# Loads and stores of a decoder block's weight parts on GpSimd's queue, and a buffer of their own for the gate rows

## The chip, the cores and the metric

One core of a Trainium2 chip runs the program. Times are device microseconds. The metric is the time of one execution, taken as the median over runs. TensorE is called PE, VectorE DVE, ScalarE ACT, GpSimd POOL and SyncE SP. Each of them takes its instructions in the order in which the built program has them; a transfer (DMA) is issued by the engine in whose order it stands, and an instruction that waits holds up those behind it on the same engine.

## The reference

The kernel computes one decoder layer on a sequence of 1024 tokens with a width of 1024, all in float32. What matters here:

```python
mod = jax.nn.silu(c) @ w_ada + b_ada            # shift, scale, gate
h = rms_norm(x, norm_gain) * (1.0 + scale) + shift
q, k, v, z_a, u, z_b, m_a, m_b = split(h @ w_in)
p_a = (stick_breaking_attention(q, k, v) * silu(z_a)) @ w_branch_a
p_b = (pool(u) * silu(z_b)) @ w_branch_b
out = (sigmoid(m_a) * p_a + sigmoid(m_b) * p_b) @ w_out
return rms_norm(x + gate * out, final_gain)
```

## The kernel before, in words

Each float32 product is made of three matmuls. An operand is split into a high part (a cast on ACT) and a low part (the operand less its high part, a subtraction on DVE or POOL), and high x high, high x low and low x high are added up in a PSUM bank. The normed input `hT` stays on the chip as high and low parts. A projection takes one tile of 128 columns of a weight (128 x 1024 numbers, 512 KB) and makes two groups of 24 matmuls, one for each half of the sequence, each into one of the two banks of the tag `pj`.

The stages follow one another on PE: maps and the projection u (to about 129 us), the values v (16 groups, to 218), the gate projection z_b, called wzb (8 tiles j = 0 to 7, two groups each, 218 to 317), the product with `w_branch_b` (seven products p1, p5, p6, p7, p4, p3, p2 of 48 matmuls each, to 394), attention mixed with the other projections (to about 1032), and the end with `w_branch_a` and `w_out`.

The projections of the attention stage use 40 tiles of `w_in`. For the first 8 the low part is made when they are used, by POOL (L118). For the other 32, the numbers 8 to 39, the low part is made ahead of time, in the stages u, v, wzb and the products, and kept in DRAM as `wl_d`; attention loads it from there. `make_lo` (L142 to L160) does this for one tile at a time: a load of the raw tile (L149, the tile `l8_raw` to `l39_raw`, tag `lraw`), the cast of it (L152, ACT, into `l_hi`, one buffer), the low part in place of the raw tile (L153, DVE), and the store (L154). A buffer of `lraw` can take the next load when its store has landed. 18 tiles are made in u and v, from the pool of buffers `vp`, which has three buffers of `lraw` and is closed at the end of v. 14 tiles are made from the pool `pb`: the code asks for four of them in the loop over wzb (`LO_ZB`) and for ten behind the seven products (`LO_PB`).

The order of each engine is not the order of the code: a scheduler places the instructions, by its own estimate of their times, in all stages in which the code doesn't pin them. So all 14 tiles of `pb` stand among the instructions of wzb.

In wzb, for each half of each tile j, ACT takes the sigmoid of the bank (L663) and DVE multiplies it with the bank (L664), which is the last reader of the bank, and then with the pooled difference (L665). The group after the next on PE writes the same bank and so waits for L664. Also in this stage DVE makes the pooled differences (L556 to L573), the low parts of the weights of wzb (L118), sums and differences of `gb` (L669 to L672), the first operands of the products (L642, L654), and the gate: one row of `w_gate` for each j (tile `wg`, loaded by L680) is multiplied with silu(c) and summed (L681). silu(c) is made once, from `sg` and `gjunk` (L675 to L678). In the kernel before, `gjunk` and the eight `wg` use the buffers of `lraw`, three in all.

SP issues nearly all loads and stores: the weights of v (L580) and of wzb (L131), the pooled input u (L557), the stores of v (L611), `wg` (L680), the halves of `w_branch_b` (L648), and L149 and L154. ACT issues a few stores. POOL issues no transfers; between 67 and 390 us it has no instruction.

Of the kernel before, what the change touches and what calls it, by code (L numbers as in the profile page):

```python
# [9 lines left out]
F32 = mybir.dt.float32  # L10
# [5 lines left out]
P = 128  # L16
D = 1024
# [23 lines left out]
LO_ZB = (0, 1, 0, 1, 0, 1, 0, 1)  # L41
LO_PB = (1, 2, 1, 2, 1, 2, 1)
# [15 lines left out]
def block_kernel(ctx, tc, a, out):  # L58
    nc = tc.nc
    v, act, gp = nc.vector, nc.scalar, nc.gpsimd  # L60

    def pool(name, **kw):
        return tc.tile_pool(name=name, bufs=1, reuse_waits="tile", **kw)
# [9 lines left out]
    def bank(tag, name):  # L73
        return psp.tile([P, 512], F32, tag=tag, bufs=BANKS[tag], name=name)
# [8 lines left out]
    wl_d = dram.tile([5 * KB, P, D], F32, name="wl_d")  # L83
# [51 lines left out]
    tiles = []  # L135
# [6 lines left out]
    def make_lo(pl, n, bufs=3, later=False):  # L142

        rest = []
        for _ in range(n):
            i = next(early_lo)
            raw = pl.tile([P, D], F32, tag="lraw", bufs=bufs, name=f"l{i}_raw")
            hi = pl.tile([P, D], F32R, tag="lhi", bufs=1, name=f"l{i}_hi")
            nc.sync.dma_start(raw, a["w_in"][tiles[i]])  # L149

            def low(i=i, raw=raw, hi=hi):
                act.copy(hi, raw)  # L152
                v.tensor_sub(raw.bitcast(F32R), raw, hi.bitcast(F32))  # L153
                nc.sync.dma_start(wl_d[i], raw)  # L154

            if later:
                rest.append(low)
            else:
                low()
        return rest  # L160
# [27 lines left out]
    def project(ct, name, use, he, le):  # L188
        whl = load_w(a["w_in"][ct], name, he, le)
        for sh in range(2):  # L190
            ps = bank("pj", f"{name}_{sh}")
            mm3(ps, whl, (h_hi, h_lo), range(KB), hmov(sh))
            use(sh, ps)
# [18 lines left out]
    with pool("init") as init:  # L212
# [101 lines left out]
        wg, maps, halves = {}, {}, {}  # L314
# [239 lines left out]
    def load_u(j):  # L554
        u = dif.tile([P, S + 16], F32, tag="u", bufs=2, name=f"u{j}")
        v.memset(u[:, S:], 0.0)  # L556
        nc.sync.dma_start(u[:, :S], u_d[j])  # L557
        return u

    def make_d(j, u):  # L560
        win = WINDOWS[j // 2]
        cur, n, step = u, S + 16, 1
        while step < win:
            nxt = dif.tile([P, S + 16], F32, tag="win", bufs=2, name=f"win{j}_{step}")
            n -= step
            v.tensor_add(nxt[:, :n], cur[:, :n], cur[:, step:step + n])
            cur, step = nxt, 2 * step
        t0 = S - win + 1
        d = dif.tile([P, S], F32, tag="d", bufs=5, name=f"d{j}")
        v.scalar_tensor_tensor(d[:, :t0], cur[:, :t0], 1.0 / win, u[:, :t0], ALU.mult, ALU.subtract)  # L570
        tl = dif.tile([P, 16], F32, tag="tl", bufs=2, name=f"tl{j}")
        v.tensor_mul(tl[:, :win - 1], cur[:, t0:S], invn[:, 16 - win + 1:])
        v.tensor_sub(d[:, t0:], tl[:, :win - 1], u[:, t0:S])  # L573
        dhls[j] = d


    with pool("vp") as vp:
# [6 lines left out]
        for i in reversed(range(KB)):  # L584
            ps = bank("pj", f"u{i}_1")
            mm3(ps, whl[i], h, range(KB), hmov(1))
            use[i](1, ps)
            make_lo(vp, 1)
# [6 lines left out]
        for hf in range(2):  # L595
            if hf == 0:
                wv.append([load_wv(1, k2) for k2 in range(4)])
            for sb in range(8):
# [18 lines left out]
                if 8 * hf + sb in DIFFS:  # L617
                    j = DIFFS[8 * hf + sb]
# [8 lines left out]
    pb = pbs.enter_context(pool("pb"))  # L627
# [11 lines left out]
    def b_op(src, name):  # L639
        hl = pb.tile([P, 2, 2, 512], F32R, tag="bhl", bufs=3, name=name)  # L640
        act.copy(hl[:, 0], src)
        v.tensor_sub(hl[:, 1], src, hl[:, 0].bitcast(F32))  # L642
        return hl
# [7 lines left out]
    def a_op(src, name):  # L651
        hl = wts.tile([P, 2, 2, 512], F32R, tag="whl", bufs=2, name=name)
        act.copy(hl[:, 0], src)
        v.tensor_sub(hl[:, 1], src, hl[:, 0].bitcast(F32))  # L654
        return hl

    for j in range(KB):
        if j not in dhls:
            make_d(j, load_u(j))

        def silu(sh, ps):
            z = gb[:, j, sh * 512:sh * 512 + 512]
            act.activation(z, ps, AF.Sigmoid)  # L663
            v.tensor_mul(z, ps, z)  # L664
            v.scalar_tensor_tensor(z, dhls[j][:, sh * 512:sh * 512 + 512], psc_v[:, j:j + 1], z, ALU.mult, ALU.mult)  # L665

        project(CZB + j, f"wzb{j}", silu, act, v)
        if j < 4:
            v.tensor_sub(t1[:, j], gb[:, j, 512:], gb[:, j, :512])  # L669
        else:  # L670
            v.tensor_sub(t2[:, j - 4], gb[:, j, 512:], t1[:, j - 4])
            v.tensor_sub(gb[:, j - 4, 512:], gb[:, j, 512:], gb[:, j - 4, 512:])  # L672
        make_lo(pb, LO_ZB[j])
        if j == 0:
            nc.sync.dma_start(sg, a["c_row"].broadcast_to([P, D]))  # L675
            gjunk = pb.tile([P, D], F32, tag="lraw", bufs=3, name="gjunk")
            act.activation(gjunk, sg, AF.Sigmoid)
            v.tensor_mul(sg, sg, gjunk)  # L678
        wg = pb.tile([P, D], F32, tag="lraw", bufs=3, name=f"wg{j}")
        nc.sync.dma_start(wg, a["w_gate"][j])  # L680
        v.scalar_tensor_tensor(wg, wg, 1.0, sg, ALU.mult, ALU.mult, accum_out=gate[:, j:j + 1])  # L681
        del dhls[j]
# [50 lines left out]
    def out_b(j, n, t):  # L733
        nc.sync.dma_start(pb_d[j][:, 512 * n:512 * n + 512], t)

    def copied(tag, bufs, j, src):
        t = sums.tile([P, 512], F32, tag=tag, bufs=bufs, name=f"{tag}_{j}")
        act.copy(t, src)
        return t

    def added(t, src):
        v.tensor_add(t, src, t)
        return t

    for n, (name, a_of, b_of) in enumerate(products):
        c = {"p5": "b", "p3": "b", "p2": "c"}.get(name, "a")
        if c not in chain:
            chain[c] = [bank((tb if c == "b" else ta)[j], f"{name}_{j}") for j in range(4)]
        ps = chain[c]
        for q in range(2):  # L750
            wl_, ml_ = a_op(a_of(q), f"{name}a{q}"), b_op(b_of(q), f"{name}b{q}")
            for j in range(4):
                for e in range(2):
                    for i, (w, m) in enumerate(((0, 0), (0, 1), (1, 0))):
                        mm(
                            ps[j], wl_[:, w, e, j * P:(j + 1) * P], ml_[:, m, e],
                            start=name in ("p1", "p5", "p2") and (q, e, i) == (0, 0, 0), stop=(q, e, i) == (1, 1, 2),
                                skip_group_check=True,
                        )
        for j in range(4):  # L760
            if name == "p1":
                keep["s1", j] = copied("s1", 4, j, ps[j])
            elif name == "p6":
                keep["s2", j] = copied("s2", 4, j, ps[j])
            elif name == "p7":
                out_b(j + 4, 1, added(copied("s3", 2, j, ps[j]), chain["b"][j]))
            elif name == "p4":
                out_b(j + 4, 0, copied("s4", 2, j, ps[j]))
            elif name == "p3":
                out_b(j, 1, added(keep["s2", j], ps[j]))  # L770
            elif name == "p2":
                out_b(j, 0, added(keep["s1", j], ps[j]))
        make_lo(pb, LO_PB[n])
    pbs.close()


# [295 lines left out]
    with pool("fin") as fin:  # L1072
# [14 lines left out]
        for sh in range(2):  # L1087
            sl = slice(sh * 512, sh * 512 + 512)
            ms = []
            for j in range(KB):  # L1090
# [9 lines left out]
                n = 0  # L1100
# [12 lines left out]
            for i in range(4):  # L1113
# [8 lines left out]
                for c_, cl in enumerate(pieces):  # L1122
                    w_ = cl.stop - cl.start
                    ps = bank(("z", "tr")[c_ % 2], f"o{sb}_{c_}")[:, :w_]
                    n = 0
# [85 lines left out]
```

## Time and profile before

| | us |
|---|---|
| median of 3 runs | 1214.39 (1213.62 to 1216.64) |
| the profiled execution | 1216.13 |
| its span, first to last instruction | 1214.4 |
| PE busy | 1193.9 (98%) |
| DVE busy | 796.0 (66%) |
| ACT busy | 549.3 (45%) |
| POOL busy | 168.8 (14%) |
| mean granted clock of PE | 0.996 |

A row of a timeline gives the start, the busy time, the engine, the line, the operation, the tiles (out<-in), the shapes and the count; the brackets give the idle time before it and what ended that. Instructions overlap a little, so the distance between two starts (1.14 for an operation over 1024 columns on DVE) is less than the busy time (1.22). In a row of stages the numbers are the length, the busy time and count of PE, weight loads, DVE, ACT and POOL, the granted clock, the busy share of the DMA engines and the GB/s. A row of transfers gives the issuer, the count, the size and the median time from issue to landing.

### The profile page before, as it was taken

To read this page: it belongs to the slowest core of one execution; us is meant where nothing else is said; L and a number is where in the kernel's file an instruction comes from. 1 tells how busy PE (TensorE), PEld (TensorE's weight loads), DVE (VectorE), ACT (ScalarE), POOL (GpSimd) and SP (SyncE) were. 2 spreads that over 40 slices of the span, in tenths; PEclk is the share of its full clock that TensorE was granted. 3 is DMA by queue.
4 is the path that set the end of the run, shared out by engine and by line. 5 is a ranking of instruction groups with operands and counts; after the bars stand their busy time and mean duration, and the time that the engine had idled before them with its cause. 6 is when DMAs were issued, how large, how long until landed. Compare 5 with 4: busy or idle time off the path is not lost.

```text
span 1214.4 us, 16128 instructions
## 1 busy us (share of the span) xinstructions
PE 1193.9 (98%) x5698; PEld 995.1 (82%) x5698; DVE 796.0 (66%) x1088; ACT 549.3 (45%) x1020; POOL 168.8 (14%) x352
## 2 busy tenths in 40 slices
PE   8999999998999999999999999999999999999997
PEld 7888788876888888888888888888888888888876
DVE  5754473696765186777858678686777753785643
ACT  5564231332453255655655655555655653232211
POOL 1000000000000333222222221222221210000001
PEclk9999999998999999999999999999999999999999
DMA  9648895687725732343534325353353235984622
GB/s 355 253 172 320 317 364 211 215 261 210 268 86 187 229 81 72 116 129 99 165 114 141 106 88 165 109 157 106 107 140 100 96 124 195 335 276 162 208 73 83
DMA packets 85699, 212.39 MB, mean 175 GB/s; under 512 B 10609, under 2 KB 24049, under 8 KB 83442
## 3 DMA queue, kind: packets, MB, share of 16 engines
q1 hardware_dynamic: 77410, 196.47, 49.3%
q10 hardware_dynamic: 8208, 14.88, 3.3%
q8 instruction: 45, 0.74, 0.2%
q14 instruction: 36, 0.29, 0.1%
HBM read 144.20 MB, written 50.34 MB: 160 GB/s over the span
## 4 chain that ended last, share of the span: by engine, by line
PE 83%; DMA 7%; DVE 5%; issue 2%; ACT 1%; POOL 0%; SPq 0%; POOLq 0%; DVEq 0%; ACTq 0%
PE p L103 43%; PE o L103 6%; PE av L103 6%; PE z L103 6%; PE wt L103 5%; PE v L103 5%; PE pa L103 5%; DMA wl_d<-l_raw 3%; PE ua L103 3%; PE wzb L103 2%; DMA l_raw<-in_w_in 2%; PE u L103 2%; PE wm L103 1%; DVE l_raw L153 1%; DMA m<-sb_d 1%
## 5 line engine op out<-in xcount | busy, mean ns | idle before, releaser
L103 PE MATMUL p<-hT,w 128*128 128x512 f32 x1920 | 479.7, 391 | 0.0
L103 PEld LDWEIGHTS p<-hT,w 128*128 128x128 f32 x1920 | 355.3, 188 | 73.8 <-DVE klo L103 0.2
L933 DVE TENSOR_TENSOR_SCAN om<-om 128x512 f32<-128x512 f32 (+7 forms) x128 | 175.5, 1371 | 123.8 <-ACT om L926 69.0
L926 ACT ACTIVATE om<-z 128x512 f32<-128x512 f32 (+2 forms) x192 | 94.6, 493 | 156.0 <-PE z L103 133.2
L952 ACT CAST wt<-wt 128x512 fp32r<-128x512 f32 (+1 forms) x160 | 88.2, 551 | 48.1 <-PE wt L103 47.9
L953 DVE TENSOR_TENSOR wt<-wt,wt 128x512 fp32r<-128x512 f32 (+1 forms) x160 | 99.3, 620 | 16.1 <-ACT wt L952 15.5
L103 PE MATMUL av<-wt,vv 128*128 128x512 f32 x320 | 106.4, 414 | 0.0
L931 POOL TENSOR_SCALAR_AFFINE_SELECT om<-om 128x128 f32<-128x128 f32 x128 | 57.3, 448 | 345.6 <-ACT om L926 286.2
L103 PE MATMUL wzb<-hT,wzb 128*128 128x512 f32 x384 | 91.3, 399 | 8.4 <-DVE gb L664 8.4
L103 DVE TENSOR_TENSOR be<-be,om 128x511 f32<-128x511 f32 (+7 forms) x128 | 95.2, 749 | 1.1 <-POOL be L931 0.7
L103 PEld LDWEIGHTS wzb<-hT,wzb 128*128 128x128 f32 x384 | 73.7, 193 | 25.8 <-DVE gb L664 10.3
L927 ACT ACTIVATE be<-z 128x512 f32<-128x512 f32 (+2 forms) x192 | 94.0, 490 | 0.0
L103 PE MATMUL pa<-ga,wa 128*128 128x512 f32 x384 | 89.9, 390 | 1.0 <-DVE s L1105 1.0
L103 PE MATMUL o<-wo,mhl 128*128 128x512 f32 (+1 forms) x408 | 89.6, 377 | 0.0
L103 PE MATMUL wt<-ident,be 128*128 128x128 f32 x576 | 89.4, 273 | 0.0
L103 PE MATMUL v<-wv,hT 128*128 128x512 f32 x384 | 88.1, 390 | 1.2 <-DVE vo L610 1.2
L103 PEld LDWEIGHTS v<-wv,hT 128*128 128x128 f32 x384 | 71.9, 188 | 17.2 <-DVE vo L610 2.3
L103 PEld LDWEIGHTS pa<-ga,wa 128*128 128x128 f32 x384 | 71.9, 188 | 16.7 <-issue 1.3
L103 PEld LDWEIGHTS o<-wo,mhl 128*128 128x128 f32 x408 | 73.5, 188 | 14.1
L103 PEld LDWEIGHTS wt<-ident,be 128*128 128x128 f32 x576 | 70.2, 141 | 11.6
L152 ACT CAST l_hi<-l_raw 128x1024 fp32r<-128x1024 f32 x32 | 33.7, 1052 | 80.5 <-DMA l_raw<-in_w_in 74.4
L153 DVE TENSOR_TENSOR l_raw<-l_raw,l_hi 128x1024 fp32r<-128x1024 f32 x32 | 39.2, 1224 | 44.1 <-ACT l_hi L152 43.9
(175 smaller groups left out, 1476.5 us busy)
## 6 DMA issues: line engine op xcount, KB each, us to landing
w_raw<-in_w_in SPq DMA_DIRECT2D x40, 512.0 KB, 4.5
l_raw<-in_w_in SPq DMA_DIRECT2D x32, 512.0 KB, 5.3
wl_d<-l_raw SPq DMA_DIRECT2D x32, 512.0 KB, 5.9
w<-wl_d SPq DMA_DIRECT2D x32, 512.0 KB, 3.8
v_d<-vo SPq DMA_DIRECT2D x16, 512.0 KB, 4.8
vv<-v_d SPq DMA_DIRECT2D x8, 1024.0 KB, 5.4
wa_raw<-in_w_branch_a SPq DMA_DIRECT2D x16, 512.0 KB, 4.7
wa<-in_w_mod SPq DMA_DIRECT2D x7, 1024.0 KB, 7.3
```

The source lines that it names most:

```text
L103: ins = op(*args, **kw)
L152: act.copy(hi, raw)
L153: v.tensor_sub(raw.bitcast(F32R), raw, hi.bitcast(F32))
L926: act.activation(om[:, b0:b0 + n], zp[:, :n], AF.Sigmoid, scale=-0.125)
L927: act.activation(be[:, b0:b0 + n], zp[:, :n], AF.Sigmoid, scale=0.125)
L931: gp.affine_select(out=tl[:, :P], in_=tl[:, :P], pattern=[[1, P]], compare_op=ALU.is_gt, fill=fill, base=0, channel_multiplier=-1)
L933: v.tensor_tensor_scan(om[:, :W], om[:, :W], om[:, :W], 1.0, ALU.mult, ALU.min)
L952: act.copy(wt[:, 0, :off], pt[:, :off])
L953: v.tensor_sub(wt[:, 1, :off], pt[:, :off], wt[:, 0, :off].bitcast(F32))
```

## The change

```diff
@@ make_lo
-            nc.sync.dma_start(raw, a["w_in"][tiles[i]])
+            gp.dma_start(raw, a["w_in"][tiles[i]])
...
-                nc.sync.dma_start(wl_d[i], raw)
+                gp.dma_start(wl_d[i], raw)
@@ the loop over wzb
-        make_lo(pb, LO_ZB[j])
+        make_lo(pb, LO_ZB[j], 2)
...
-            gjunk = pb.tile([P, D], F32, tag="lraw", bufs=3, name="gjunk")
+            gjunk = pb.tile([P, D], F32, tag="wg", bufs=1, name="gjunk")
...
-        wg = pb.tile([P, D], F32, tag="lraw", bufs=3, name=f"wg{j}")
+        wg = pb.tile([P, D], F32, tag="wg", bufs=1, name=f"wg{j}")
@@ behind each product
-        make_lo(pb, LO_PB[n])
+        make_lo(pb, LO_PB[n], 2)
```

L149 and L154 are issued by POOL in place of SP, in all 32 rounds. In `pb`, `lraw` has two buffers in place of three, and `gjunk` and the `wg` share one of their own; the space is the same. Line numbers stay as they are.

The scheduler places the instructions anew. PE's order is the same. On SP, at the start of wzb, before:

```order
L680 DMA wg0_1798<-in_w_gate 128x1024
L149 DMA l26_raw_1863<-in_w_in 128x1024
L680 DMA wg1_1869<-in_w_gate 128x1024
L680 DMA wg2_1934<-in_w_gate 128x1024
L131 DMA wzb4_raw_2022<-in_w_in 128x1024
L149 DMA l27_raw_1999<-in_w_in 128x1024
L557 DMA u7_2256<-u_d_78 128x1024
L154 DMA wl_d_79<-l26_raw_1863 128x1024
```

Now, at the same place, SP has the gate rows, the weights and u alone:

```order
L680 DMA wg0_1798<-in_w_gate 128x1024
L131 DMA wzb4_raw_2022<-in_w_in 128x1024
L680 DMA wg1_1869<-in_w_gate 128x1024
L557 DMA u7_2256<-u_d_78 128x1024
L680 DMA wg2_1934<-in_w_gate 128x1024
L131 DMA wzb5_raw_2102<-in_w_in 128x1024
L680 DMA wg3_2005<-in_w_gate 128x1024
```

POOL had nothing between L255 and the L118 of the first attention weights. It now has the loads and stores of the tiles, here from the first of `pb` on:

```order
L149 DMA l26_raw_1863<-in_w_in 128x1024
L149 DMA l27_raw_1999<-in_w_in 128x1024
L154 DMA wl_d_79<-l26_raw_1863 128x1024
L149 DMA l28_raw_2165<-in_w_in 128x1024
L154 DMA wl_d_79<-l27_raw_1999 128x1024
L149 DMA l29_raw_2335<-in_w_in 128x1024
L154 DMA wl_d_79<-l28_raw_2165 128x1024
L149 DMA l30_raw_2427<-in_w_in 128x1024
```

Load and store alternate: the load of a tile stands between the stores of the two tiles before it, and it goes on like this to l39. The next on POOL are the L118 of the first attention weights.

On DVE, at the end of wzb, before (`wzb6_1` is the bank of the second half of tile 6):

```order
L153 TENSOR_TENSOR l37_raw_2855<-l37_raw_2855,l37_hi_2856 128x1024
L153 TENSOR_TENSOR l38_raw_2861<-l38_raw_2861,l38_hi_2862 128x1024
L664 TENSOR_TENSOR gb_1725<-wzb6_1_2223,gb_1725 128x512
L665 SCALAR_TENSOR_TENSOR gb_1725<-d6_2185,vecs_89,gb_1725 128x512
L654 TENSOR_TENSOR p1a0_2357<-a11_0_2355,p1a0_2357 128x1024
L671 TENSOR_TENSOR t2_1727<-gb_1725,t1_1726 128x512
L672 TENSOR_TENSOR gb_1725<-gb_1725 128x512
L153 TENSOR_TENSOR l39_raw_2943<-l39_raw_2943,l39_hi_2944 128x1024
L664 TENSOR_TENSOR gb_1725<-wzb7_0_2277,gb_1725 128x512
L665 SCALAR_TENSOR_TENSOR gb_1725<-d7_2267,vecs_89,gb_1725 128x512
L664 TENSOR_TENSOR gb_1725<-wzb7_1_2305,gb_1725 128x512
```

And now:

```order
L153 TENSOR_TENSOR l37_raw_2855<-l37_raw_2855,l37_hi_2856 128x1024
L664 TENSOR_TENSOR gb_1725<-wzb6_1_2223,gb_1725 128x512
L665 SCALAR_TENSOR_TENSOR gb_1725<-d6_2185,vecs_89,gb_1725 128x512
L654 TENSOR_TENSOR p1a0_2357<-a11_0_2355,p1a0_2357 128x1024
L671 TENSOR_TENSOR t2_1727<-gb_1725,t1_1726 128x512
L672 TENSOR_TENSOR gb_1725<-gb_1725 128x512
L153 TENSOR_TENSOR l38_raw_2861<-l38_raw_2861,l38_hi_2862 128x1024
L664 TENSOR_TENSOR gb_1725<-wzb7_0_2277,gb_1725 128x512
L665 SCALAR_TENSOR_TENSOR gb_1725<-d7_2267,vecs_89,gb_1725 128x512
L153 TENSOR_TENSOR l39_raw_2943<-l39_raw_2943,l39_hi_2944 128x1024
L664 TENSOR_TENSOR gb_1725<-wzb7_1_2305,gb_1725 128x512
L665 SCALAR_TENSOR_TENSOR gb_1725<-d7_2267,vecs_89,gb_1725 128x512
```

l38 and l39 stand one group later; l26 stands at the start of the stage, right behind L678, where the first L681 stood. In between, from l28 to l39, one new L153 stands ahead of each L664 except that of wzb2_1. The eight L681 stand later than before, the last ahead of L664 of wzb5_0 in place of wzb3_0.

## The prediction

> **What bounds the kernel now.** I read the page first, then who waited for whom, then the timelines of PE and DVE, then the chain in order of time.
>
> ```profile
> span 1214.4 us, 16128 instructions
> PE 1193.9 (98%) x5698; PEld 995.1 (82%) x5698; DVE 796.0 (66%) x1088; ACT 549.3 (45%) x1020; POOL 168.8 (14%) x352
> ...
> q1 hardware_dynamic: 77410, 196.47, 49.3%
> q10 hardware_dynamic: 8208, 14.88, 3.3%
> ```
>
> PE is busy for 98% of the span, so what a change of queues can win is a part of the 20.5 us in which it is idle. The waits of PE say where those are, and its timeline says when.
>
> ```profile
> PE wzb L103 <- DVE gb L664: 8.4, 4, 4.4
> PE v L103 <- DVE vo L610: 1.2, 2, 1.0
> ```
>
> ```profile
> 217.99 38.24 PE L103 MATMUL wzb<-hT,wzb 128*128 128x512 f32 x168
> 257.73 5.74 PE L103 MATMUL wzb<-hT,wzb 128*128 128x512 f32 x24 [1.50 <-DVE gb L664]
> 264.79 11.17 PE L103 MATMUL wzb<-hT,wzb 128*128 128x512 f32 x48 [1.32 <-DVE gb L664]
> 277.14 16.79 PE L103 MATMUL wzb<-hT,wzb 128*128 128x512 f32 x72 [1.19 <-DVE gb L664]
> 298.29 19.35 PE L103 MATMUL wzb<-hT,wzb 128*128 128x512 f32 x72 [4.36 <-DVE gb L664]
> 317.48 11.17 PE L103 MATMUL p<-p1b,p1a 128*128 128x512 f32 x48
> ```
>
> The wzb stage has 16 groups of 24 matmuls. The first seven take 38.24, so 5.46 each, and 16 would take 87.4; the stage takes 317.48 - 217.99 = 99.5. Four waits make 8.4 of the difference. The last also costs clock: 72 matmuls take 16.79 before it and 19.35 after it, 2.6 more, while the granted clock (last number but two) falls.
>
> ```profile
> 256.00:288.00 32.00, 27.99 (x121) 22.30 (x120) 28.86 (x39) 11.68 (x14) 0.00 (x0) 1.00 0.72 181
> 298.00:302.00 4.00, 3.71 (x9) 2.94 (x10) 3.57 (x6) 1.32 (x2) 0.00 (x0) 0.50 0.92 304
> ```
>
> The waits of 1.2 to 1.5 left it at 1.00; the one of 4.36 halved it. All these waits end with L664 on DVE, which frees the bank. Why L664 is late stands in the chain in order of time and in DVE's timeline.
>
> ```profile
> 241.12 5.22 DMA wl_d<-l_raw
> 246.35 3.57 DMA l_raw<-in_w_in
> ...
> 250.00 1.06 ACT l_hi L152
> ...
> 251.08 0.14 DVE l_raw L153
> ```
>
> ```profile
> 227.07 1.23 DVE L678 TENSOR_TENSOR sg<-sg,gjunk 128x1024 f32<-128x1024 f32 x1 [1.34 <-ACT gjunk L677]
> 228.33 1.22 DVE L681 SCALAR_TENSOR_TENSOR wg<-wg,sg 128x1024 f32<-128x1024 f32 x1
> ...
> 229.70 0.69 DVE L664 TENSOR_TENSOR gb<-wzb,gb 128x512 f32<-128x512 f32 x1
> ...
> 235.18 1.22 DVE L153 TENSOR_TENSOR l_raw<-l_raw,l_hi 128x1024 fp32r<-128x1024 f32 x1
> ...
> 239.26 1.23 DVE L153 TENSOR_TENSOR l_raw<-l_raw,l_hi 128x1024 fp32r<-128x1024 f32 x1
> ...
> 243.95 1.22 DVE L118 TENSOR_TENSOR wzb<-wzb_raw,wzb 128x1024 fp32r<-128x1024 f32 x1
> 245.09 1.22 DVE L642 TENSOR_TENSOR p1b<-gb,p1b 128x1024 fp32r<-128x1024 f32 x1
> ```
>
> ```profile
> 313.57 1.22 DVE L153 TENSOR_TENSOR l_raw<-l_raw,l_hi 128x1024 fp32r<-128x1024 f32 x1
> 314.70 0.69 DVE L664 TENSOR_TENSOR gb<-wzb,gb 128x512 f32<-128x512 f32 x1
> 315.43 0.75 DVE L665 SCALAR_TENSOR_TENSOR gb<-d,vecs,gb 128x512 f32<-128x512 f32 x1
> 318.31 0.69 DVE L664 TENSOR_TENSOR gb<-wzb,gb 128x512 f32<-128x512 f32 x1 [2.13 <-ACT gb L663]
> 319.04 0.75 DVE L665 SCALAR_TENSOR_TENSOR gb<-d,vecs,gb 128x512 f32<-128x512 f32 x1
> 319.70 1.22 DVE L654 TENSOR_TENSOR p1a<-a,p1a 128x1024 fp32r<-128x1024 f32 x1
> ```
>
> A raw tile goes round: store, load into its buffer, cast on ACT, low part (L153) on DVE, store. DVE takes its instructions in order, so an L664 behind an L153 waits for that round. From l27 (239.26) to l39 (313.57) twelve tiles come at 6.2 us each, slower than PE's 5.46 per group, and PE falls back to their pace.
>
> **The change part by part.**
>
> *Where the L153 stand.* In the order of DVE, l38 stood ahead of L664 of group wzb6_1 and stands now ahead of wzb7_0; l39 stood ahead of wzb7_0 and stands now ahead of wzb7_1. From l28 on each stands ahead of an L664 of its own. The same lateness of l39 thus costs one group (5.46) less. That is the gain; whether it stays depends on the pace of the tiles.
>
> *The pace.* On POOL, load k+2 stands ahead of store k+1 and waits for store k, since there are two buffers in place of three. The round of two tiles is s + l + 1.16 (landing to L153) + 1.24 (L153 to store). For s and l, issue to landing, I take the medians (last number) from SP's queue, first in this stage, then in the V stage, which is used below.
>
> ```profile
> l_raw<-in_w_in SPq DMA_DIRECT2D x14, 512.0 KB, 4.5
> wl_d<-l_raw SPq DMA_DIRECT2D x14, 512.0 KB, 4.8
> wg<-in_w_gate SPq DMA_DIRECT2D x8, 512.0 KB, 4.4
> ```
>
> ```profile
> wl_d<-l_raw SPq DMA_DIRECT2D x12, 512.0 KB, 6.1
> l_raw<-in_w_in SPq DMA_DIRECT2D x10, 512.0 KB, 6.3
> ```
>
> No transfer is issued from POOL in this trace (the page's two queues of transfers are SP's q1 and ACT's q10), so what its issue adds to each transfer, x, is unknown. Bounds: -0.6, if l falls from 4.5 to near the 3.57 in the chain because SP's other transfers no longer stand ahead; and 2.4, what POOL takes for an operation over a tile of this size. The nearest row is POOL's shortest arithmetic of a column, 0.55, since an issue works on addresses and not on the tile. I take x = 0.6.
>
> ```profile
> 64.35 0.55 POOL L255 TENSOR_TENSOR st<-st,mhalf 128x1 f32<-128x1 f32 x1 [0.51 <-ACT junk L103]
> 390.23 2.42 POOL L118 TENSOR_TENSOR w<-w_raw,w 128x1024 fp32r<-128x1024 f32 x1 [322.87 <-ACT w L123]
> ```
>
> The round is then 5.4 + 5.1 + 2.4 = 12.9 for two tiles, 6.45 for one. (The Trainium skill, "DMA: Bandwidth & Descriptors", section "Latency and other measured facts", gives about 1 us to the first byte from GpSimd and 0.6 from SP; by that x would be 0.4, and the end below 2 us earlier. No run here shows it yet.)
>
> *The walk.* l26 now follows the L678 of 227.07, where the first L681 stood: 228.3, its store issues at 229.6 and lands at 235.0; load 28 lands at 240.1, L153 of l28 at 241.2. DVE is there at 241.0, after l27 at 235.0 (the rows from 229.70 to 235.18 stand unchanged between them, 5.5) and 1.14 + 4.85 more (L664, L566, L681, L665, L566). Behind l28 stand L664, L118, L566, L642, L681, L665, L572, L566: about 1.14 for the long ones (243.95 to 245.09), 7.1 in all, so L153 of l29 comes at 249.5, by DVE and not by its load (246.7 + 1.2). From there the round sets it: l31 262.4, l33 275.3, l35 288.2, l37 301.1, l39 314.0. Behind l39: L153 1.13, L664 and L665 1.3 and L654 1.2, so the second half of p1 can start at 317.7. Before it started at 317.48 + 5.50 = 323.0. Gain: 5.3.
>
> *PE beside it.* L664 of wzb6_1 ends at 302.9, group wzb7_1 runs to 308.4, the first half of p1 to 313.9; then PE waits 3.8 for L654. That lies between the waits that kept the clock and the one that lost 2.6; I count half, 1.3. (By the Trainium skill, "TensorE: Matmul & The Clock Gate", "What's actually happening", the clock falls after an idle window of about 3.4 us that runs freely, so 3.8 would cost it only at times; the 4.36 above agrees.) Net gain 4.0.
>
> *The V stage.* There are three buffers still, so a tile costs (6.1 + 6.3 + 2.4 + 1.2) / 3 = 5.3, a V group 5.5:
>
> ```profile
> L103 PE MATMUL v<-wv,hT 128*128 128x512 f32 x384 | 88.1, 390 | 1.2 <-DVE vo L610 1.2
> ```
>
> At most one L153 stands ahead of an L610 from the second group on but for one pair, and a bank gives about 4 us of grace. I count nothing, between the 1.2 that can go and some 4 lost if x is 2.4.
>
> *SP without 64 issues.* 0.33 each makes 21 us of SP's time, and waits like the one below go from its queue. Nothing that PE waits for is issued late by SP in these stages, so I count nothing.
>
> ```profile
> SPq L149 <- DMA wl_d<-l_raw: 55.9, 21, 7.7
> ```
>
> *wg in one buffer.* A load of 4.4 and an L681 of 1.2 make, with their issue, about 6; the eight L681 are spread over groups 1 to 10, mostly with two groups between. Hidden; where one group lies between, at most 0.6 late, within the grace.
>
> *POOL's other work.* The next instruction there is the L118 of 390.23. The last store issues near 315: 70 us of cover, nothing.
>
> **The rivals.**
>
> *POOL's issue costs nothing* (x near 0, or below, as loads no longer queue behind wg and wzb). The end moves by ten transfers (five stores, five loads from l29 to l39), 10 us per us of x: 311.7 at x = 0, near the 310.9 that PE needs for 87.4 + 5.46, and no clock is lost. 1214.4 - 11.3 - a part of the 1.2 = 1202.5. For it: the 3.57 against the median 4.5. Against it: one queue more shares the same engines, busy 0.72 and 0.92 of the two windows above.
>
> *Only issue time is saved.* The 55.9 are waits for data, not for a free queue: SP stood there because the store had not landed, and the same wait stands on POOL. If the pace of 6.2 becomes about 6.8 with two buffers (x = 1.0 with the clock kept, or 0.9 with it lost), the group is eaten: 1214. (The Trainium skill, "DMA: Bandwidth & Descriptors", "Issuing engines are not separate DMA queues", says the same: the engines behind are shared, and only the issue is saved.)
>
> *Slower: POOL's issue is late beside a busy DVE.* DVE is busy 28.86 of 32 us here. If POOL can write a transfer's list only between DVE's instructions, it waits for one of 1.22 on top of 0.6: x = 1.8, the end at 329.7, the clock lost (2.6), so 9.3 later than before, and 1 or 2 in the V stage: 1225. It turns to a loss that can be told from x = 1.2 on. (The Trainium skill, "SBUF — State Buffer", "Who interferes with whom", has this lock for copies and the like on DVE, and infers that tensor_tensor leaves the write side free; nothing here shows which.) Against it: DVE runs TENSOR_TENSOR and SCALAR_TENSOR_TENSOR here, and no copies.
>
> **How the numbers follow.** The profiled execution took 1216.13 with a span of 1214.4; the median of the runs is 1214.39. A shift in the span moves both alike. Chances: forecast 0.42, at 1214.4 - 4.0 = 1210.4 (from x = 0.3, clock kept, 1206, to x = 0.9, clock lost, 1215); issue for nothing 0.23, 1202.5; only issue time 0.15, 1214; slower 0.20, 1225, from 1218 (x = 1.2) up. The range that leaves out 2 in 10 is 1202 to 1222. About 0.3% (3.6 us) is what a measurement can tell here: faster than 1210.8 takes all of the second case and two thirds of the first (0.28), 0.51; within it the rest of the first and most of the third, 0.28; slower 0.21.
>
> **What would show it.** Right: a queue of POOL in the page; L153 in pairs of rounds of about 12.9 us; l39 near 314, p1 from about 308.4; PE's waits in wzb below 1.5 each and one of about 4 at p1's second half. The size is wrong if the round is under 12 or over 14; the idea is wrong if L664 no longer waits for an L153 and PE waits all the same, or if the V stage grows by more than 2.

## The result and the profile after

The changed kernel takes 1222.43 us in the median of 5 runs, beside 1213.89 for the kernel before: a ratio of 1.0070, with a 95% interval of 1.0043 to 1.0098. It is slower by 0.4 to 1.0%. The forecast was 1210.4, faster by 0.3%, in a range up to 1222.0. A second measurement, among the experiments, gave 1.0062 (1.0040 to 1.0084).

The profiled execution took 1224.54, the longest of the five. The page of it has a queue that the page of before had not, q0, which carries what POOL issues:

```profile
span 1222.8 us, 16140 instructions
PE 1196.0 (98%) x5698; PEld 996.4 (81%) x5698; DVE 796.8 (65%) x1088; ACT 549.1 (45%) x1020; POOL 202.4 (17%) x416
...
q0 software_dynamic: 9216, 33.56, 7.6%
```

PE's waits, longest in total first, are the same waits as before, and longer, with one new line (p):

```profile
PE wzb L103 <- DVE gb L664: 10.9, 5, 5.4
PE v L103 <- DVE vo L610: 2.4, 2, 1.9
PE p L103 <- DVE gb L664: 2.3, 1, 2.3
```

PE's timeline says where the 8.4 us between the two spans arise. The wzb stage starts at 220.60 in place of 217.99, p1 at 322.80 in place of 317.48, and p5 at 336.38 in place of 328.48. From there to the end both kernels take about 886 (885.9 and 886.4), so 7.9 of the 8.4 lie ahead of p5.

```profile
220.60 32.80 PE L103 MATMUL wzb<-hT,wzb 128*128 128x512 f32 x144
...
309.16 13.80 PE L103 MATMUL wzb<-hT,wzb 128*128 128x512 f32 x48 [5.38 <-DVE gb L664]
322.80 4.30 PE L103 MATMUL p<-p1b,p1a 128*128 128x512 f32 x18
329.40 7.15 PE L103 MATMUL p<-p1b,p1a 128*128 128x512 f32 x30 [2.29 <-DVE gb L664]
336.38 11.15 PE L103 MATMUL p<-p5b,p5a 128*128 128x512 f32 x48
```

The rows below are the L153 of l32, l33, l35, l36, l38 and l39 in DVE's timeline. Up to l32 none of the tiles finds DVE idle. Three of the later ones come late, behind an idle time of DVE: l33 9.61 behind l32, l36 12.28 behind l35, and l39 8.84 behind l38, where a tile was to take 6.45.

```profile
272.05 1.23 DVE L153 TENSOR_TENSOR l_raw<-l_raw,l_hi 128x1024 fp32r<-128x1024 f32 x1
281.66 1.22 DVE L153 TENSOR_TENSOR l_raw<-l_raw,l_hi 128x1024 fp32r<-128x1024 f32 x1 [3.57 <-ACT l_hi L152]
...
295.00 1.23 DVE L153 TENSOR_TENSOR l_raw<-l_raw,l_hi 128x1024 fp32r<-128x1024 f32 x1 [2.40 <-ACT l_hi L152]
...
307.28 1.22 DVE L153 TENSOR_TENSOR l_raw<-l_raw,l_hi 128x1024 fp32r<-128x1024 f32 x1 [6.66 <-ACT l_hi L152]
...
318.67 1.23 DVE L153 TENSOR_TENSOR l_raw<-l_raw,l_hi 128x1024 fp32r<-128x1024 f32 x1 [0.43 <-ACT l_hi L152]
...
327.51 1.23 DVE L153 TENSOR_TENSOR l_raw<-l_raw,l_hi 128x1024 fp32r<-128x1024 f32 x1 [6.23 <-ACT l_hi L152]
```

The chain in order of time runs through the same places. From 261 on its transfers (start, length from issue to landing) take between 3.6 and 8.5 us. The four long ones and one of the short ones:

```profile
273.58 8.22 DMA wl_d<-l_raw
...
289.94 8.15 DMA wl_d<-l_raw
...
299.08 8.52 DMA wl_d<-l_raw
...
308.80 4.62 DMA wl_d<-l_raw
...
319.07 7.28 DMA l_raw<-in_w_in
```

What was in their way is seen in the lists of transfers by stretch. In the stretch around l36 there is one more transfer, the store of the gate sums (L684), issued at 292.63: 4 KB, and 10.7 us to land. While it is under way little moves. From 296 to 300 the DMA engines (the last two numbers of the row are their busy share and GB/s) are idle, and up to 304 they move 36 GB/s, though a load and a store of POOL's are queued from 298.37 and 299.08 on.

```profile
g_d<-gate SPq DMA_DIRECT2D x1, 4.0 KB, 10.7
```

```profile
296.00:300.00 4.00, 4.00 (x20) 3.30 (x19) 3.96 (x7) 0.40 (x1) 1.09 (x2) 1.00 0.00 0
300.00:304.00 4.00, 3.77 (x17) 2.81 (x15) 0.62 (x2) 0.00 (x0) 0.00 (x0) 1.00 0.28 36
```

The kernel before has the same store, issued at 268.31, and it is as slow there. A load of wzb's weights issued behind it took as long:

```profile
wzb_raw<-in_w_in SPq DMA_DIRECT2D x1, 512.0 KB, 10.7
...
g_d<-gate SPq DMA_DIRECT2D x1, 4.0 KB, 10.1
```

Neither the prediction nor its rivals has this store. So there were three theories to test. A: two buffers in place of three cost the time. B: POOL's queue costs it. C: the gate store costs it, because the change moves it among the last tiles. A fourth arose on the way: loads that SP sends ahead.

### The profile page after: what moved, and what is told of

It is laid out like the page before. It is cut to its first block, busy times and chain, and to the rows that moved or that the text cites. A ratio compares the mean times of both kernels' runs of the same rounds, so it can differ in the third digit from the quotient of the medians.

```text
span 1222.8 us, 16140 instructions
## 1 busy us (share of the span) xinstructions
PE 1196.0 (98%) x5698; PEld 996.4 (81%) x5698; DVE 796.8 (65%) x1088; ACT 549.1 (45%) x1020; POOL 202.4 (17%) x416
## 4 chain that ended last, share of the span: by engine, by line
PE 76%; DMA 10%; issue 8%; DVE 3%; ACT 1%; POOL 1%; SPq 0%; POOLq 0%; ACTq 0%; DVEq 0%
PE p L103 40%; PE o L103 6%; PE av L103 6%; PE z L103 6%; PE wt L103 5%; PE pa L103 5%; DMA wl_d<-l_raw 4%; PE ua L103 3%; PE v L103 2%; PE u L103 2%; DMA l_raw<-in_w_in 2%; PE wm L103 1%; DMA m<-sb_d 1%; DMA kh<-kh 1%; DVE l_raw L153 1%
## 5 line engine op out<-in xcount | busy, mean ns | idle before, releaser
L153 DVE TENSOR_TENSOR l_raw<-l_raw,l_hi 128x1024 fp32r<-128x1024 f32 x32 | 39.1, 1222 | 40.9 <-ACT l_hi L152 40.9
```

## The experiments

Each kernel ran beside the kernel before on the same chip. Ratios are to that kernel, with 95% intervals.

**One half of the change each.** split_only has the buffers of the change and all transfers on SP:

```diff
-            gp.dma_start(raw, a["w_in"][tiles[i]])
+            nc.sync.dma_start(raw, a["w_in"][tiles[i]])
...
-                gp.dma_start(wl_d[i], raw)
+                nc.sync.dma_start(wl_d[i], raw)
```

> The buffers split as in the change (two for the raw tiles, one for the gate rows), all transfers still on SP. Theory A, two buffers instead of three cost the time and POOL's queue next to nothing: about 1222, within 3, with L153 at some 7 us each from the stage's start to l39. Theory B, POOL's queue costs the time (its loads land in 6.5 in the median): 1214 or less, about 1210 as forecast without x. Theory C, the late 4 KB store of the gate sums (10.7 us to land in the changed kernel) costs it: between them, about 1218, if that store is again issued after 290 us.

Measured: 1.0024 (1.0013 to 1.0036). The gate store is issued at 290.38, and l37 comes 12.5 behind l36, as l36 comes 12.28 behind l35 in the changed kernel. pool_only is the other half, the first hunk of the change alone:

```diff
-            nc.sync.dma_start(raw, a["w_in"][tiles[i]])
+            gp.dma_start(raw, a["w_in"][tiles[i]])
...
-                nc.sync.dma_start(wl_d[i], raw)
+                gp.dma_start(wl_d[i], raw)
```

> Transfers of the low tiles on POOL, three buffers shared with the gate rows as before. Theory A: 1210 to 1215, the last six L153 at about 4.7 us each as before. Theory B: 1220 or more, PE's waits for L664 above 10 us in the wzb stage. Theory C: as before, since the gate rows are loaded as before and their store is issued near 270 us.

Measured: 1.0019 (1.0005 to 1.0033). Neither A nor B alone explains 0.7%: each half has a small cost, and the sum, 0.43%, is at the lower end of what the whole costs.

A half is more than its edit, since the scheduler places the instructions anew each time. In pool_only the last tiles stand on DVE as in the changed kernel (l39 ahead of wzb7_1); in split_only l39 stands ahead of wzb7_0, as before. And in pool_only, alone of the kernels so far, PE's order has changed too: the first four matmuls of p1 stand ahead of the last group of wzb.

**The gate store, moved.** gate_late_after is the changed kernel with the store behind p6; a small DVE operation on p6's result holds it there.

```diff
-    nc.sync.dma_start(g_d[0].rearrange("(k p) -> p k", p=P), gate)
...
                 keep["s2", j] = copied("s2", 4, j, ps[j])
+                if j == 0:
+                    v.scalar_tensor_tensor(gate, keep["s2", 0][:, :KB], 0.0, gate, ALU.mult, ALU.add)
+                    nc.sync.dma_start(g_d[0].rearrange("(k p) -> p k", p=P), gate)
```

> The changed kernel with the 4 KB store of the gate sums moved behind p6 (a 128x8 operation on DVE makes it wait). Theory A: 1219 to 1223, since the round of two buffers sets the pace anyway. Theory C: about 1216: the wait for l36 of 6.66 falls to 2, the end of the stage comes 4.6 earlier and 1.3 of lost clock stays. Theory B: 1222.

Measured: 1.0041 (1.0029 to 1.0053). The long wait for l36 is gone. From the start of wzb to p5 PE takes 114.4 (216.69 to 331.07) in place of 115.8, and of 118.2 in a repeat of the changed kernel. But the store now lands in 13.4 beside the loads for p4, and PE waits 1.2 and 1.5 there. gate_far_after moves it on into the attention stage and keeps the sums in a new tile of 32 bytes among the constants:

```diff
+    gkeep = const.tile([P, KB], F32, name="gkeep")
...
-    v.tensor_add(gate, gate, bias)
+    v.tensor_add(gkeep, gate, bias)
...
                 nc.sync.dma_start(ga_d[p][:, sl], tp)
+                if (p, t) == (2, 0):
+                    v.scalar_tensor_tensor(gkeep, tp[:, :KB], 0.0, gkeep, ALU.mult, ALU.add)
+                    nc.sync.dma_start(g_d[0].rearrange("(k p) -> p k", p=P), gkeep)
```

> The changed kernel with the 4 KB store of the gate sums moved far back, into the attention stage (third pair, after its first product with za), where the trace shows only loads made well ahead. If that store's 10 us cost what the wait for l36 shows: 4 to 5 below the changed kernel, about 1218. If the round of two buffers eats it: within 2 of the changed kernel, 1220 to 1223.

Measured: 1.0056 (1.0038 to 1.0073), no gain that can be told. The stretch from wzb's start to p5 was 4.0 shorter than in a repeat of the changed kernel, but other stages were longer, without a wait. PE's groups show it: a pa matmul took 396 ns in place of 389 (first the repeat of the changed kernel, then this one; 32 bytes ahead of all tiles had moved every address).

```profile
L103 PE MATMUL pa<-ga,wa 128*128 128x512 f32 x384 | 89.6, 389 | 0.1
```

```profile
L104 PE MATMUL pa<-ga,wa 128*128 128x512 f32 x384 | 92.4, 396 | 0.1
```

So the same was done with the sums in a tile that stands there unused, and no address moves: gate_far2_after from the changed kernel, gate_far_before from the kernel before.

```diff
-    const.tile([P, 24], F32, name="skip")
+    gkeep = const.tile([P, 24], F32, name="skip")
```

> The changed kernel with the 4 KB store of the gate sums in the attention stage again, the sums kept in an unused tile, so that no other tile's address moves (the earlier kernel of this kind had 32 more bytes ahead of all tiles, and its pa matmuls took 396 ns in the mean instead of 389). If the store's place costs the 4.0 that the stretch from the wzb stage's start to p5 lost in the profiles: ratio to before 1.002 to 1.004, about 4 under the changed kernel. If the time isn't won after all: 1.006 again.

> The kernel before with the same move of the store. There it is issued at 268.31, while three buffers stand and DVE still has other work. If only the changed kernel meets it: within 1 us of before. If it costs before as well (the last waits of 1.19 and 4.36 come behind it): 3 to 5 faster.

Measured: 1.0012 (1.0003 to 1.0021) for the changed kernel, and 0.9934 (0.9921 to 0.9947) for the kernel before. The store costs 0.5% in the one and 0.7% in the other. As an explanation of the difference between the two kernels, C falls: with the store gone from both, they are still 0.78% apart. As an explanation of the wait of 4.36 in the kernel before, it stands. In gate_far_before PE has no wait at all from 277.25 to p1 (first fence, PE), the wzb stage takes 94.2 (216.10 to 310.32) in place of 99.5, and the last seven tiles take 4.4 each (second, DVE: l29, l32 and l39). From 272 to 280, where the store was under way in the kernel before, the DMA engines now move 184 GB/s in place of 66 (the last two rows: the kernel before, then gate_far_before):

```profile
277.25 33.23 PE L103 MATMUL wzb<-hT,wzb 128*128 128x512 f32 x144 [1.15 <-DVE gb L664]
310.32 11.17 PE L103 MATMUL p<-p1b,p1a 128*128 128x512 f32 x48
```

```profile
261.21 1.22 DVE L153 TENSOR_TENSOR l_raw<-l_raw,l_hi 128x1024 fp32r<-128x1024 f32 x1
...
277.72 1.21 DVE L153 TENSOR_TENSOR l_raw<-l_raw,l_hi 128x1024 fp32r<-128x1024 f32 x1
...
308.24 1.23 DVE L153 TENSOR_TENSOR l_raw<-l_raw,l_hi 128x1024 fp32r<-128x1024 f32 x1 [0.44 <-ACT l_hi L152]
```

```profile
272.00:280.00 8.00, 6.81 (x31) 5.32 (x29) 8.00 (x11) 2.75 (x4) 0.00 (x0) 1.00 0.78 66
```

```profile
272.00:280.00 8.00, 6.85 (x31) 5.35 (x30) 8.00 (x11) 3.72 (x5) 0.00 (x0) 1.00 0.51 184
```

In gate_far2_after, DVE's L153 of l29, l32, l38 and l39: from l32 to l38 six tiles in 39.4, a round of 13.1, and then 10.29 for a single tile. From l29 to l39 it is 7.0 a tile, a round of 14.0.

```profile
250.92 1.22 DVE L153 TENSOR_TENSOR l_raw<-l_raw,l_hi 128x1024 fp32r<-128x1024 f32 x1
...
271.26 1.22 DVE L153 TENSOR_TENSOR l_raw<-l_raw,l_hi 128x1024 fp32r<-128x1024 f32 x1 [0.93 <-ACT l_hi L152]
...
310.63 1.23 DVE L153 TENSOR_TENSOR l_raw<-l_raw,l_hi 128x1024 fp32r<-128x1024 f32 x1 [0.88 <-ACT l_hi L152]
...
320.92 1.23 DVE L153 TENSOR_TENSOR l_raw<-l_raw,l_hi 128x1024 fp32r<-128x1024 f32 x1 [7.67 <-ACT l_hi L152]
```

**The store's elements.** Its 1024 elements of 4 bytes go to 1024 places. gate_rows_before keeps the far store and adds one more at the old place, the same bytes as rows of 32:

```diff
+    g2_d = dram.tile([P, KB], F32, name="g2_d")
...
     v.tensor_add(gkeep[:, :KB], gate, bias)
+    nc.sync.dma_start(g2_d, gkeep[:, :KB])
```

> gate_far_before with one store more: the same 128x8 sums go to a scratch tensor of rows of 32 bytes, at the old place in SP's queue (behind the low tile's store near 268), beside the far store of single elements. If the 1024 elements of 4 bytes are what makes the store take 10 us and block the others: this one lands in 2 to 3 us and the ratio stays 0.993. If any store at that place costs it: 0.998 to 1.000.

Measured: 0.9962 (0.9947 to 0.9978), 1208.41 us beside the 1208.25 of gate_far_before on another chip. The ratio lies between the two expectations; the trace decides for the elements, since the store lands in 3.8, behind it wzb's load takes 4.2, the two stores of tiles around it take 4.3 in the median, and PE has no wait from 275.09 to p1:

```profile
wl_d<-l_raw SPq DMA_DIRECT2D x2, 512.0 KB, 4.3
wzb_raw<-in_w_in SPq DMA_DIRECT2D x1, 512.0 KB, 4.2
g_d<-skip SPq DMA_DIRECT2D x1, 4.0 KB, 3.8
```

**Loads that run ahead.** l39's load takes 7.28 in the changed kernel. Just ahead of it SP issues three loads of w_branch_b, 1.5 MB, in 1.6 us:

```profile
317.06 0.88 SPq L648 DMA_DIRECT2D a<-in_w_branch_b  x2
318.04 0.57 SPq L648 DMA_DIRECT2D a11s<-in_w_branch_b  x1
```

In the kernel before SP had to issue the low tiles too, and the last two of these loads went out at 315.18 and 315.71, behind l39's load of 308.83. a_on_pool is the changed kernel with these loads on POOL, where they stand behind l39's load:

```diff
-        nc.sync.dma_start(raw, a["w_branch_b"][r0:r0 + 2 * P, 512 * m:512 * m + 512].rearrange("(k p) c -> p k c", p=P))
+        gp.dma_start(raw, a["w_branch_b"][r0:r0 + 2 * P, 512 * m:512 * m + 512].rearrange("(k p) c -> p k c", p=P))
```

> The changed kernel with the loads of w_branch_b's tiles on POOL too, where they stand behind the last low tile's load instead of running ahead of it on SP. If those three loads made l39's load late (7.3 and 8.0 from issue to landing in the two profiles): it lands in about 4.5, p1's second half starts some 3 earlier, ratio to before about 1.004. If not: 1.006.

Measured: 1.0037 (1.0025 to 1.0050). The last two loads of low tiles land in 4.5 in the median:

```profile
l_raw<-in_w_in POOLq DMA_DIRECT2D x2, 512.0 KB, 4.5
```

So l39's load was late because of these loads. What that is worth is less sure. By the medians it is 0.29% (1.0037 in place of 1.0066, the mean of the two measurements of the changed kernel), but the intervals overlap. Nor do the profiles decide it: PE waits 0.26 in p1 in place of 2.29, but 7.34 for l36 in place of 5.38. From the start of wzb to p5 it takes 116.6 here (216.62 to 333.25), 115.8 in the first profile of the changed kernel and 118.2 in the second.

after_far_a_pool has this edit and the far store:

> The changed kernel, gate store far back, and w_branch_b's loads on POOL behind the last low tile's. If both parts add (0.0054 and 0.0029 each off the changed kernel's 1.0066): 0.998 to 0.999. If both only shorten the same wait (p1's second half, 6.26 in gate_far2_after): no better than 0.9995.

Measured: 0.9999 (0.9988 to 1.0009), 0.13% under gate_far2_after; the intervals overlap, so whether the two parts add is unclear. With both out of the way the changed kernel is still 0.65% slower than gate_far_before, so these two parts do not make up the difference.

**The halves again, with the store out of the way.** split_gate_far and pool_gate_far are split_only and pool_only with the far store.

> Buffers split (two and one), all on SP, gate store far back. The part of the two buffers alone, with the store out of the way. From the paces in the profiles (a tile of the last six in 6.5 with two buffers on SP, 4.5 with three): the last tiles end some 5 later than in gate_far_before, of which half shows at p5: ratio to before 0.996 to 0.998. If the buffers are the whole difference: 1.001, as gate_far2_after.

> Low tiles on POOL, three shared buffers, gate store far back. The part of the queue alone. At 0.5 us more per tile and with w_branch_b's loads ahead of the last one: 0.995 to 0.997. If the queue is the whole difference: 1.001; if it is none of it: 0.993.

Measured: 0.9965 (0.9953 to 0.9978) and 0.9980 (0.9967 to 0.9992). From gate_far_before's 0.9934 that is +0.31% for the buffers and +0.46% for the queue; the sum, 0.77%, is what gate_far2_after shows (+0.78%). The sizes are less sure than this fit. gate_far_before ran on another chip; counted from gate_rows_before (0.9962), which ran on the chip of the two halves, they are +0.03% and +0.18%. And pool_gate_far has PE's order of pool_only: PE waits at p1's first matmuls for ACT and takes the last group of wzb after them.

```profile
305.46 1.39 PE L103 MATMUL p<-p1b,p1a 128*128 128x512 f32 x4 [1.90 <-ACT p1a L653]
306.65 7.09 PE L103 MATMUL wzb<-hT,wzb 128*128 128x512 f32 x24
```

A price of the queue with PE's order kept (DVE's is not) is seen between kernels with two buffers: 0.42% from split_only to the changed kernel and 0.47% from split_gate_far to gate_far2_after. The intervals lie apart, though the chips differ here too.

The profiles show how the two act. From the L153 of l29 to that of l39 a tile takes 4.7 in gate_far_before (261.21 to 308.24), 5.3 in pool_gate_far (262.26 to 315.21), 6.4 in split_gate_far (244.46 to 308.24) and 7.0 in gate_far2_after (250.92 to 320.92), beside PE's 5.46 a group. With two buffers on SP a tile takes longer, but the gate rows have their own buffer and the tiles start earlier, so l39 comes 93.1 after the stage's start, beside 92.1 in gate_far_before. With two buffers on POOL it is 103.1. From the start of wzb to p5 PE takes 105.2, 108.0, 106.7 and 114.9 in this order: in these single executions the two halves together cost more than their sum.

The landings from 225 to 325, in the order gate_far_before (three buffers, SP), pool_gate_far (three, POOL), split_gate_far (two, SP), gate_far2_after (two, POOL):

```profile
wl_d<-l_raw SPq DMA_DIRECT2D x14, 512.0 KB, 4.8
l_raw<-in_w_in SPq DMA_DIRECT2D x13, 512.0 KB, 4.5
```

```profile
wl_d<-l_raw POOLq DMA_DIRECT2D x14, 512.0 KB, 4.7
l_raw<-in_w_in POOLq DMA_DIRECT2D x13, 512.0 KB, 4.9
```

```profile
wl_d<-l_raw SPq DMA_DIRECT2D x14, 512.0 KB, 4.3
l_raw<-in_w_in SPq DMA_DIRECT2D x12, 512.0 KB, 4.0
```

```profile
wl_d<-l_raw POOLq DMA_DIRECT2D x14, 512.0 KB, 5.7
l_raw<-in_w_in POOLq DMA_DIRECT2D x12, 512.0 KB, 4.9
```

A store and a load together take 9.3 and 9.6 with three buffers, and 8.3 and 10.6 with two. By these medians POOL's x is 0.15 a transfer in the one case and 1.15 in the other. But the rows do not count the same loads (13, 13, 12 and 12). As means over l28 to l39, where a trace has the landing, x is 0.67 with three buffers and 0.61 with two.

**Low tiles with three buffers to themselves.** wg_in_raw puts the gate rows into the two buffers of the weights' raw tiles, all on SP:

```diff
-        wg = pb.tile([P, D], F32, tag="lraw", bufs=3, name=f"wg{j}")
+        wg = wts.tile([P, D], F32, tag="raw", bufs=2, name=f"wg{j}")
```

> All on SP; the gate rows take the two buffers of the weights' raw tiles, so the low tiles have three buffers to themselves. Theory A: 1203 to 1210, faster than before, L153 at about 5 us each. Theory B: says nothing of buffers, 1210 to 1214. Theory C: depends only on where the gate store comes; 1212 to 1216.

Measured: 1.0006 (0.9995 to 1.0016). The tiles come at 4.9 each and l39 at 289.43, as A has it; but the gate rows hold up wzb's own weights, and PE waits 5.4 and 2.3 for these, early in the stage. t2_sp puts the rows into t2 instead, which is free until the fifth tile of wzb, two rows per tile of wzb; t2_pool is the same on POOL:

```diff
-        wg = pb.tile([P, D], F32, tag="lraw", bufs=3, name=f"wg{j}")
...
+        for r in (2 * j, 2 * j + 1) if j < 4 else ():
+            wg = t2[:, 2 * (r % 2):2 * (r % 2) + 2].rearrange("p a c -> p (a c)")
```

> All on SP, three buffers for the low tiles alone; the gate rows (two per pair of groups, done by the eighth group) lie in t2, which is free until then. If the few buffers cost the time: L153 at about 5 us each, the last before 295, the wzb stage without its 8.4 of waits and 2.6 of lost clock, so 1203 to 1206. If the waits had another cause: 1211 or more.

> The same with the low tiles' transfers on POOL. If POOL's queue adds some 0.5 us per tile (as between the first runs) and three free buffers hide it: within 2 of t2_sp, 1203 to 1208. If POOL's queue costs time that buffers don't hide: 4 or more above t2_sp.

Measured: 0.9973 (0.9960 to 0.9986) and 1.0006 (0.9994 to 1.0018). Three free buffers win 0.27% on SP, less than expected, with L153 still at 6.1 us each (228.11 to 307.65), and with POOL's queue it is 0.33% more, so free buffers don't hide its cost. (Here it is t2_sp in which p1's first matmuls stand ahead of the last group of wzb, and t2_pool in which they don't.) In both the gate store takes 13.5 and 14.4 in the midst of the tiles. t2_sp_gate_far moves it:

> Low tiles alone in three buffers, all on SP, gate rows in t2, and the gate store far back. In t2_sp the store landed in 13.46 and a low tile's store beside it in 9.49. If the parts add: 3 to 4 faster than t2_sp, ratio to before about 0.994. If the order of DVE sets the pace there (its L153 stand unwaited up to 280): as t2_sp, 0.997.

Measured: 0.9930 (0.9918 to 0.9941), 1207.3 us in place of 1215.46. That beats both kernels, but gate_far_before, with the store moved and nothing else, is as fast within the intervals: with the store gone the three shared buffers are enough.

**The changed kernel once more.**

> The changed kernel itself once more, beside the others. 1220 to 1224. If the 2.6 by which its V stage grew in the first profile is scatter, the stage takes about 88 here (it took 88.6 in the kernel with the late gate store, whose order is the same up to there); if it is a price of POOL's queue, about 91 again.

Measured: 1.0062 (1.0040 to 1.0084). Its V stage takes 88.0 (128.21 to 216.23) where the first profile had 91.7 with the same instructions, and before had 89.1. The 2.6 by which wzb started later is scatter of one execution.

## Why the prediction was wrong, point by point

- **"PE falls back to their pace."** This failed first. The 6.2 is no pace but a mean of two. In the kernel before, l27 to l29 take 21.8 for two tiles (239.26 to the row below), while gate rows take turns in the same buffers; the ten tiles from l29 to l39 take 5.2 each, and 4.7 in gate_far_before. That is below PE's 5.46. What made the wait of 4.36 is the gate store: without it the wait is gone. The trace of before has the row of that store, 4 KB and 10.1 to land; the prediction rested on the rows of 512 KB alone. So a round of two buffers, 6.45 a tile, was no small step from 6.2, but one from below PE's pace to above it.

```profile
261.10 1.22 DVE L153 TENSOR_TENSOR l_raw<-l_raw,l_hi 128x1024 fp32r<-128x1024 f32 x1
```

- **"Before it started at 317.48 + 5.50 = 323.0. Gain: 5.3."** The step that gave the sign. The walk for the changed kernel used undisturbed landings, and was set against a time of before that had the store's delay in it. Counted from the start of wzb, the walk's 317.7 is 99.7 and the 323.0 of before 105.0; gate_far_before, without the delay, has 310.32 + 5.5 - 216.10 = 99.7. Like against like, the walk had no gain. The changed kernel itself has 329.40 - 220.60 = 108.8.
- **"The round is then 5.4 + 5.1 + 2.4 = 12.9."** Nearly right: in gate_far2_after 13.1 from l32 to l38 and 14.0 in the mean from l29 to l39; on SP, in split_gate_far, 12.8. In the changed kernel l39 came at 327.51 in place of 314.0. Of the 13.5, 2.6 is the later start of the stage, and three tiles at 9.61, 12.28 and 8.84 in place of 6.45 make 11.4; the other tiles together gained 0.5. PE's waits in wzb were to be below 1.5 each; the longest is 5.38, and the 48 matmuls behind it take 13.80, not 11.17.
- **"wg in one buffer ... Hidden."** The L681 are hidden, as argued. What stands behind the last of them is not: the store of the sums is issued at 292.63 in place of 268.31, and meets l36.
- **"Nothing that PE waits for is issued late by SP ... I count nothing."** True, and the wrong question. What SP no longer holds back goes out early: 1.5 MB ahead of l39's load (8.84 for that tile). Taking it away won 0.29% by the medians, with intervals that overlap.
- **x = 0.6.** Right, as far as it can be told: 0.67 and 0.61 by the means, though 0.15 and 1.15 by the medians. The rounds of 14.0 on POOL and 12.8 on SP, two transfers each, give 0.6 too. The cost of POOL's queue was not what the prediction had wrong.
- **The order's gain of one group** could not be tried alone, since the scheduler makes the order from the same choices. By DVE's order in the traces the later place of l38 and l39 comes with POOL's queue: pool_only and pool_gate_far have it, split_only and split_gate_far do not. What it is worth stays open.
- **The V stage, POOL's other work**: nothing, as counted (88.0 for V in the repeat, 89.1 before).
- **The rivals.** The time is that of the slower rival (1225), but its mechanism did not show. Its x was 1.8, and the rounds show 0.6. POOL's issue rows for the low tiles have one length (0.53 to 0.56 but for the first, 0.77), beside a busy DVE as beside an idle one. These two are from 257.72, where DVE works without a gap, and from 298.37, where it idles:

```profile
257.72 0.54 POOL L149 DMA_DIRECT2D l_raw<-in_w_in  x1 [2.96 <-DMA wl_d<-l_raw]
...
298.37 0.54 POOL L149 DMA_DIRECT2D l_raw<-in_w_in  x1 [7.90 <-DMA wl_d<-l_raw]
```

  "Only issue time is saved" had the right idea, a pace near the old one with the group eaten, and the wrong size. The Trainium skill, "DMA: Bandwidth & Descriptors", section "Issuing engines are not separate DMA queues", says that more issuing engines save only the issue. The runs go beyond it: on POOL the same transfers cost between 0.2 and 0.5%.

What causes the loss, then: the buffers and POOL's queue, and each is shown to cost something by a half of its own (1.0013 to 1.0036 and 1.0005 to 1.0033). Together they bring the last ten tiles from below PE's pace to above it (4.7 to 7.0 a tile). How the 0.7% divides is not settled: 0.03 to 0.3% for the buffers and 0.2 to 0.5% for the queue, and in the profiles both together cost more than the sum. Each part includes what the scheduler's new order does. That the store delayed l36, and the early loads l39, is shown; how much of the 0.7% they are is not, since without both the difference is 0.65%. Why l33's load took 8.91 is open too: it was issued within 2.6 us of a gate row, wzb's weights and a tile's store.

## What to carry to other kernels

Before a lateness is called the pace of a loop, look whether it holds in every part of the stretch, and for any transfer whose landing is out of proportion to its size. Here the mean hid two paces, and a store of scattered single elements held up the transfers beside it. When the time before is compared with a walk of the time after, both must hold the same disturbances. A queue kept in order also holds back what stands behind it: when its work is moved elsewhere, list what now goes out early and whom it meets.

## What the runs showed of the hardware

- A store of 1024 single elements of 4 bytes took 9.4 to 14.4 us to land (10.1 before, 10.7 in the changed kernel), and transfers of its own queue and of POOL's were late beside it (10.7, 7.7 and 8.5 for 512 KB). The same 4 KB in rows of 32 bytes took 3.8. The Trainium skill, "DMA: Bandwidth & Descriptors", section "Back-pressure in remote DMA", says of transfers between cores that stalled writes stall the other queues of the same DMA engine. The idle row from 296 to 300 would fit that for transfers inside one core; no run here shows what stalled.
- A load or store of 512 KB of a low tile, issued from POOL, held POOL for 0.54 us in place of SP's 0.33, beside a busy DVE and beside an idle one. The loads of `w_branch_b` held it for about 0.72.
- In the one profile with a tile of 32 bytes ahead of all others, which moved the addresses behind it, pa's matmuls took 396 ns and u's 397, with the granted clock at 1.00 in the pa stage. In every other profile they take 389 or 390 and 392 or 393, that of the kernel with the same instructions and unmoved addresses among them.
